# First LayerNorm's rows as background steps and a wider pace for the adaLN loads in a two-layer DiT kernel

## The chip, the cores and the metric

One core of a Trainium2 chip runs the kernel. The metric is the device time of one execution in microseconds, the median over several runs. An engine is one of the core's units: PE (TensorE, products), DVE (VectorE), ACT (ScalarE), POOL (GpSimd) and SP (SyncE, which here only issues DMAs).

## What is computed

The reference is two layers of a diffusion transformer block on 256 latent tokens and 256 context tokens with D = 1024. Cut to what the change touches:

```python
for l in range(DEPTH):                                        # DEPTH = 2
    mod_lat = silu(c) @ w_ada[l] + b_ada[l]                   # adaLN: 6 x 1024 shifts, scales and gates
    sh1, sc1, g1, sh2, sc2, g2 = split(mod_lat, 6)            # and the same for the context from c_ctx
    o_lat, o_ctx = token_mixer(x * (1 + sc1) + sh1, ...)      # attention, recurrence, output projection
    x = layernorm(ALPHA * x + g1 * o_lat, ln1_g[l], ln1_b[l])
    x = layernorm(ALPHA * x + g2 * mlp(x * (1 + sc2) + sh2), ln2_g[l], ln2_b[l])
    # mlp(h) = square(relu(h @ w_ff1)) @ w_ff2, hidden width 4096
    # in layer 0 the same two steps for the context; the output is the latent part after layer 1
```

## The kernel before, in words

**Tiles.** x is held as four blocks of 128 tokens (0 and 1 context, 2 and 3 latent), each as two halves of 128x512. Layer 0 works on all 512 tokens, layer 1's MLP on the 256 latent ones. Every product is made as three fp32r products of high and low halves (hi by hi, hi by lo, lo by hi). Weights come in units of 1 MB (tile `raw`): ACT casts a unit's four pieces to the high half `whi` (L120), DVE subtracts to the low half `wlo` (L128). Of `raw` there are three buffers, of split units two, so SP's next weight load waits until an earlier unit is split. A unit's split is emitted in four pieces between the matmuls of the unit before it.

**The MLP** (`mlp`, L1348). `f1(q, ns)` makes quarter q of the hidden layer in four units, transposed (`ps_cm`), and `ff1_evac` takes the relu and its square on ACT and splits it on DVE into `f_hi` and `f_lo` (L122 and L128). `f2(q)` multiplies a quarter by four units of the second matrix (`ps_tm`); where q < 3 it first calls f1 for one unit of the next quarter. In layer 0 a unit is 48 matmuls of 512 columns, 16 units in f1 and 16 in f2. The residual adds gate times result to x: L1180 (`res`) on DVE, L1181 (`x<-x,res`) on POOL, in the last quarter on DVE, with the statistics of the second LayerNorm behind (L1183).

**The first LayerNorm.** `ln_z` normalises x (L1219), `ln_t` transposes it on PE (`ps_z`), and `ln_h` makes the MLP's input h_hi and h_lo from that, with the rows g and b folded into scale and shift. The residual, though, needs x itself times g plus b. That is `ln_x` (L1249): it loads the rows g and b, each over 128 partitions (`ln_rows`, `ln_row` at L412), and for each half of a block emits a product (L1256) and a sum (L1257) on POOL, in place. In layer 0 that is 16 operations, in layer 1 eight. `mlp` calls it behind f1(0). `ln_x` also serves the second LayerNorm (`which == 2`), at the start of layer 1.

**adaLN.** The vectors of layer 1 are made in the background. `ada_queue` (L268) puts eight loads of 1 MB of w_ada (`raw_ada`, L275) into a queue, each with eight adds on DVE into eight accumulators (L290 for the first load, L292 after it); behind the eighth, `sums` makes 16 small matmuls (`ps_ada`), DVE adds the bias (L304, `ada_rows`), POOL scales the gate rows (L402) and PE transposes (`ps_adaT`). The table ADA starts two such queues at layer 0's MLP, 16 loads in all. `ada_step` is called when a unit begins; it emits the adds that are left, any sums that are due, and one load, if the planner's time has reached `ada_at`.

**What orders the work.** The planner counts PE time in `self.pe` (0.42 ns a column of a matmul). `tick`, called every three matmuls, emits a weight piece every third time, a step of the queue `bg` when `pe` has reached `bg_next`, and one ada add when it has reached `ada_next`. A step of `bg` has a cost; the next is emitted that much later. All of this sets the order of emission on each engine. At run time an instruction waits for its data, for its buffer and for its engine's earlier instructions, not for the planner's time.

```python
self.ada_at, self.ada_next, self.ada_gap = self.pe + pace, self.pe + 3000, (pace - 3000) / 8
```

Of the kernel before, what the change touches and what calls it, by code (L numbers as in the profile page):

```python
# [11 lines left out]
ALU = mybir.AluOpType  # L12
# [35 lines left out]
class Kern:  # L48
# [219 lines left out]
    def ada_queue(self, l, blocks, dve):  # L268
# [18 lines left out]
        def add(k, j, s):  # L287
            acc, w, c = st["acc"][s][j], st[k][:, j, :], self.silu[:, k, s:s + 1]
            if k == 0:
                self.nc.vector.tensor_scalar(acc, w, c, None, op0=ALU.mult)  # L290
            else:
                self.nc.vector.scalar_tensor_tensor(acc, w, c, acc, op0=ALU.mult, op1=ALU.add)  # L292
# [24 lines left out]
        for k in range(KD):  # L317
            if dve:
                self.ada_q.append((lambda k=k: dma(k),
                                   [lambda k=k, j=j, s=s: add(k, j, s) for j in range(4) for s in range(2)],  # L320
                                   sums if k == KD - 1 else None, self.ADA_PACE[l]))
            else:
                self.ada_q.append((lambda k=k: dma(k), [], lambda k=k: mms(k), 0.0))

    ADA_PACE = (9500, 10000)

    ADA = (('bra0',0,4,1),('bra0',0,8,1),('mlp0',1,0,1),('mlp0',1,4,1),('ga1',1,8,0))

# [919 lines left out]

    def ln_x(self, l, which):  # L1249

        nc = self.nc
        g, b = self.ln_rows(l, which)
        for tb in (range(4) if which == 1 and l == 0 else range(2, 4)):
            for hf in range(2):
                z = self.x[tb][hf]
                nc.gpsimd.tensor_tensor(z, z, g[hf], op=ALU.mult)  # L1256
                nc.gpsimd.tensor_tensor(z, z, b[hf], op=ALU.add)  # L1257
                if which == 2:
                    nc.sync.dma_start(out=self.xd[128 * (tb - 2):128 * (tb - 1), 512 * hf:512 * hf + 512], in_=z)

    def tail_units(self, l, which, keys, xs):

# [85 lines left out]
    def mlp(self, l):  # L1348
        cols = BOTH if l == 0 else LAT
        f = {}  # L1350

        def f1(q, ns=range(4)):
            for n in ns:
                w = self.take((l, "f1", q, n))
                for b in range(2):
                    p = self.cm_now(w, self.h, cols, b)
                    t = (self.g("f_hi", F32R), self.g("f_lo", F32R))
                    self.ff1_evac(p, cols, t)
                    f.setdefault(q, []).append(t)

        def f2(q, ns=range(2)):
            if q < 3:
                f1(q + 1, (0,))
            for n in ns:
                for h in range(2):
                    key = (l, "f2", q, n, h)
                    self.unit(key, self.take(key), f[q], self.tbs, q == 3)
            if q < 3:
                f.pop(q)
                f1(q + 1, (1, 2, 3))  # L1370

        self.start_residual(l, 2)
        if l == 0:

            ws = [self.take((l, "f1", 0, 0)), self.take((l, "f1", 0, 1), prefetch=False)]
            f[0] = [(self.g("f_hi", F32R), self.g("f_lo", F32R)) for _ in range(4)]
            for c in (CTX, LAT):
                for j in range(2):
                    if c is LAT and j:
                        self.prefetch()  # L1380
                    for b in range(2):
                        self.ff1_evac(self.cm_now(ws[j], self.h, c, b), c, f[0][2 * j + b])
                    if c is CTX and not j:
                        self.ln_late()
            f1(0, (2, 3))
        else:
            f1(0)
        self.ln_x(l, 1)
        for q in range(3):
            f2(q)  # L1390
        self.h = None
        f2(3, (0,))
        self.tail_units(l, 2, [(l, "f2", 3, 1, 0), (l, "f2", 3, 1, 1)], f[3])

# [174 lines left out]
```

## Time and profile before

| | before |
|---|---|
| median of 3 runs | 1557.56 us (1554.78 to 1559.41) |
| profiled execution | 1555.25 us |
| its span in the profile | 1553.4 us |
| PE busy | 1485.0 us, 96% |
| DVE busy | 1209 us, 78% |
| ACT busy | 723.8 us, 47% |
| POOL busy | 293.1 us, 19% |
| mean granted clock of PE | 0.979 |

The span is the stretch that the profile covers in the one execution that it recorded. Busy is the time in which an engine had an instruction in work; the granted clock is the share of full speed that TensorE had. Times in the trace count from the span's start. Layer 0's MLP runs from about 600 to 970 us, layer 1's from about 1363 us to the end.

### The profile page before, as it was taken

The page shows a single profiled execution, that of the slowest core. Times are in us where ns is not written, and L with a number is a line of the kernel's source. Part 1 is how long each engine was busy: PE and PEld are TensorE (multiplying, and loading weights), DVE is VectorE, ACT ScalarE, POOL GpSimd, SP SyncE. Part 2 cuts the span into 40 slices and gives each one's busy share as a digit, 9 for nine tenths or more (in the row PEclk, how much of TensorE's full clock was granted, in tenths as well). Part 3 has the DMA queues.
Part 4 walks back from the last instruction along what each step waited for, and adds up shares of the span by engine and source line. Part 5 has one row for each costly group of instructions (what it writes and reads, how often), then busy time and mean ns, then how long its engine had stood idle before and what let it go on. Part 6 is the DMA issues. An engine that isn't in the chain of part 4 may idle for free. (4 is left out here: it accounts for less than half of the span.)

```text
span 1553.4 us, 22377 instructions
## 1 busy us (share of the span) xinstructions
PE 1485.0 (96%) x8364; PEld 1231.1 (79%) x8364; DVE 1209.0 (78%) x2355; ACT 723.8 (47%) x1486; POOL 293.1 (19%) x302
## 2 busy tenths in 40 slices
PE   8799999999999999989999999899889999999997
PEld 4587988776878789866878888798777788898996
DVE  4799987849788869898984347988999756888667
ACT  2477766655224225312223232276577645555443
POOL 0532322100000002442030201445231000022110
PEclk9999999999999999989999999899899999999999
DMA  9522310014657544545552332252435723856553
GB/s 326 177 83 82 135 55 28 29 41 126 210 200 243 193 166 124 203 141 186 182 182 90 101 107 71 82 165 86 129 115 171 245 83 129 263 185 190 190 190 109
DMA packets 156750, 225.70 MB, mean 145 GB/s; under 512 B 5841, under 2 KB 118993, under 8 KB 151521
## 3 DMA queue, kind: packets, MB, share of 16 engines
q1 hardware_dynamic: 156640, 224.27, 43.9%
q8 instruction: 66, 1.08, 0.3%
q14 instruction: 44, 0.35, 0.1%
HBM read 218.97 MB, written 5.28 MB: 144 GB/s over the span
## 5 line engine op out<-in xcount | busy, mean ns | idle before, releaser
L128 DVE TENSOR_TENSOR wlo<-raw,whi 128x512 fp32r<-128x512 f32 x560 | 403.0, 744 | 119.4 <-ACT whi L120 113.6
L120 ACT CAST whi<-raw 128x512 fp32r<-128x512 f32 x483 | 275.5, 620 | 388.1 <-PE ps_tm L92 198.9
L92 PE MATMUL ps_cm<-h_hi,whi 128*128 128x256 f32 (+1 forms) x1216 | 412.7, 343 | 5.8 <-DVE whi L122 3.0
L92 PE MATMUL ps_cm<-h_hi,wlo 128*128 128x256 f32 (+1 forms) x1216 | 406.0, 336 | 3.2 <-DVE wlo L128 3.2
L92 PE MATMUL ps_cm<-h_lo,whi 128*128 128x256 f32 (+1 forms) x1216 | 406.9, 336 | 1.1 <-POOL h_lo L1241 0.8
L92 PEld LDWEIGHTS ps_cm<-h_hi,whi 128*128 128x128 f32 x1216 | 231.1, 191 | 48.8 <-issue 18.5
L92 PEld LDWEIGHTS ps_cm<-h_hi,wlo 128*128 128x128 f32 x1216 | 231.7, 191 | 27.9 <-DVE wlo L128 4.2
L92 PEld LDWEIGHTS ps_cm<-h_lo,whi 128*128 128x128 f32 x1216 | 232.4, 191 | 24.8 <-POOL h_lo L1241 2.4
L292 DVE SCALAR_TENSOR_TENSOR ada_acc<-raw_ada,silu,ada_acc 128x512 f32<-128x512 f32 x224 | 173.7, 820 | 26.7 <-DMA raw_ada<-in_w_ada_dram 26.5
L92 PE MATMUL ps_tm<-wlo,f_hi 128*128 128x512 f32 x384 | 150.8, 393 | 8.9 <-DVE wlo L128 8.9
L92 PE MATMUL ps_tm<-whi,f_hi 128*128 128x512 f32 x384 | 150.5, 392 | 0.0
L92 PE MATMUL ps_tm<-whi,f_lo 128*128 128x512 f32 x384 | 150.4, 392 | 0.0
L1181 POOL TENSOR_TENSOR x<-x,res 128x512 f32<-128x512 f32 x36 | 56.6, 1578 | 268.4 <-DVE res L1180 268.4
L92 PE MATMUL ps_tm<-wlo,h_hi 128*128 128x256 f32 x320 | 95.5, 298 | 8.0 <-DVE wlo L128 8.0
L92 PE MATMUL ps_tm<-whi,h_hi 128*128 128x256 f32 x320 | 96.9, 303 | 5.4 <-DVE whi L122 4.3
L92 PE MATMUL ps_tm<-whi,h_lo 128*128 128x256 f32 x320 | 94.4, 295 | 0.0
L92 PEld LDWEIGHTS ps_tm<-wlo,f_hi 128*128 128x128 f32 x384 | 72.8, 189 | 25.1 <-DVE wlo L128 10.2
L103 ACT ACTIVATE p<-ps_s,mx 128x512 f32<-128x512 f32 (+1 forms) x96 | 58.4, 615 | 57.8 <-DVE mx L993 29.9
L92 PEld LDWEIGHTS ps_tm<-whi,f_hi 128*128 128x128 f32 x384 | 72.7, 189 | 15.2
L92 PEld LDWEIGHTS ps_tm<-whi,f_lo 128*128 128x128 f32 x384 | 72.6, 189 | 15.1
L1241 POOL TENSOR_TENSOR h_lo<-hf,h_hi 128x256 fp32r<-128x256 f32 x28 | 23.4, 843 | 268.9 <-DVE h_hi L1240 267.8
L92 PEld LDWEIGHTS ps_tm<-wlo,h_hi 128*128 128x128 f32 x320 | 65.1, 204 | 10.6 <-DVE wlo L128 9.8
(171 smaller groups left out, 2509.8 us busy)
## 6 DMA issues: line engine op xcount, KB each, us to landing
raw<-in_w_ff_dram SPq DMA_DIRECT2D x64, 1024.0 KB, 5.5
raw<-in_w_in_dram SPq DMA_DIRECT2D x50, 1024.0 KB, 5.0
raw_ada<-in_w_ada_dram SPq DMA_DIRECT2D x40, 1024.0 KB, 4.9
w_ada<-in_w_ada_dram SPq DMA_DIRECT2D x32, 256.0 KB, 5.7
raw<-in_w_br_c_dram SPq DMA_DIRECT2D x8, 1024.0 KB, 5.2
raw<-in_w_out_dram SPq DMA_DIRECT2D x8, 1024.0 KB, 5.4
gw_raw<-in_v_gate_dram SPq DMA_DIRECT2D x16, 256.0 KB, 5.3
raw<-in_w_br_a_dram SPq DMA_DIRECT2D x8, 512.0 KB
```

The source lines that it names most:

```text
L92: self.nc.tensor.matmul(out, lhsT, rhs, start=start, stop=stop, **kw)
L103: ins = self.nc.scalar.activation(out, in_, func, **kw).ins
L120: self.nc.scalar.copy(out, in_)
L128: self.nc.vector.tensor_tensor(lo, src, hi.bitcast(F32), op=ALU.subtract)
L292: self.nc.vector.scalar_tensor_tensor(acc, w, c, acc, op0=ALU.mult, op1=ALU.add)
L1181: (nc.vector if last else nc.gpsimd).tensor_tensor(x, x, t, op=ALU.add)
L1241: last = (nc.gpsimd if s == 0 or k % 2 else nc.vector).tensor_tensor(lo[:, c], h, hi[:, c].bitcast(F32), op=ALU.subtract)
```

## The change

`ln_x` for the first LayerNorm no longer emits its operations at once: it appends each as a step of cost 2000 to `bg`, and is called ahead of f1 (in layer 0 ahead of its third and fourth unit, in layer 1 ahead of the first) instead of behind it. f1's first unit of quarter 1 is taken out of `f2(0)` and stands before it, and behind it the steps that are left are emitted (`drain_bg`). The order of PE's products stays as it was. The pace of layer 1's loads of w_ada goes from 10000 to 18000.

```diff
-    ADA_PACE = (9500, 10000)
+    ADA_PACE = (9500, 18000)
...
         for tb in (range(4) if which == 1 and l == 0 else range(2, 4)):
             for hf in range(2):
                 z = self.x[tb][hf]
+                if which == 1:
+                    for row, op in ((g[hf], ALU.mult), (b[hf], ALU.add)):
+                        self.bg.append((2000, lambda z=z, row=row, op=op: nc.gpsimd.tensor_tensor(z, z, row, op=op), False))
+                    continue
                 nc.gpsimd.tensor_tensor(z, z, g[hf], op=ALU.mult)
                 nc.gpsimd.tensor_tensor(z, z, b[hf], op=ALU.add)
-                if which == 2:
-                    nc.sync.dma_start(out=self.xd[128 * (tb - 2):128 * (tb - 1), 512 * hf:512 * hf + 512], in_=z)
+                nc.sync.dma_start(out=self.xd[128 * (tb - 2):128 * (tb - 1), 512 * hf:512 * hf + 512], in_=z)
...
         def f2(q, ns=range(2)):
-            if q < 3:
+            if 0 < q < 3:
                 f1(q + 1, (0,))
...
+            self.ln_x(l, 1)
             f1(0, (2, 3))
         else:
+            self.ln_x(l, 1)
             f1(0)
-        self.ln_x(l, 1)
         for q in range(3):
+            if q == 0:
+                f1(1, (0,))
+                self.drain_bg()
             f2(q)
```

In the changed file the first LayerNorm's operations have line 1259, those of the second 1261 and 1262.

SP's queue in the first half of layer 0's MLP, before. `raw` of 128x8x256 is a unit of f1, of 128x4x512 one of f2; the pair in the fourth row is f1(0)'s last unit and the unit of f1(1, (0,)).

```order
L275 DMA raw_ada<-in_w_ada_dram 128x2048
L412 DMA gate<-gd 128x512 x4
L275 DMA raw_ada<-in_w_ada_dram 128x2048
L186 DMA raw<-in_w_ff_dram 128x8x256 x2
L275 DMA raw_ada<-in_w_ada_dram 128x2048
L186 DMA raw<-in_w_ff_dram 128x4x512
L275 DMA raw_ada<-in_w_ada_dram 128x2048
L186 DMA raw<-in_w_ff_dram 128x4x512
L412 DMA ln_row<-in_ln_g_dram 128x512 x2
L412 DMA ln_row<-in_ln_b_dram 128x512 x2
```

And the same place of the changed kernel:

```order
L275 DMA raw_ada<-in_w_ada_dram 128x2048
L412 DMA gate<-gd 128x512 x4
L186 DMA raw<-in_w_ff_dram 128x8x256
L275 DMA raw_ada<-in_w_ada_dram 128x2048
L186 DMA raw<-in_w_ff_dram 128x8x256
L412 DMA ln_row<-in_ln_g_dram 128x512 x2
L412 DMA ln_row<-in_ln_b_dram 128x512 x2
L186 DMA raw<-in_w_ff_dram 128x4x512
L275 DMA raw_ada<-in_w_ada_dram 128x2048
L186 DMA raw<-in_w_ff_dram 128x4x512 x2
```

The rows' loads have moved ahead of two weight loads of f2 and two of w_ada, and a w_ada load now stands at every second weight load.

POOL from the end of `ln_h` to the start of layer 1, with what is taken out and put in:

```order
 L1241 TENSOR_TENSOR h_lo<-hf,h_hi 128x256 x12
-L1256 TENSOR_TENSOR x<-x,ln_row 128x512 x4
-L1257 TENSOR_TENSOR x<-x,ln_row 128x512 x4
-L1256 TENSOR_TENSOR x<-x,ln_row 128x512 x2
-L1257 TENSOR_TENSOR x<-x,ln_row 128x512 x2
-L1256 TENSOR_TENSOR x<-x,ln_row 128x512 x2
-L1257 TENSOR_TENSOR x<-x,ln_row 128x512 x2
-L1181 TENSOR_TENSOR x<-x,res 128x512 x16
+L1259 TENSOR_TENSOR x<-x,ln_row 128x512 x16
+L1181 TENSOR_TENSOR x<-x,res 128x512 x24
```

The sixteen products and sums have one line now; they stand between the same neighbours. The gate rows' product (L402), which stood among the residuals' sums, now follows them.

DVE around f1(1, (0,)) and the first units of f2, before. The adds are those of the w_ada loads; the first wlo is the last piece of f2's first unit, the next three are of its second:

```order
L128 TENSOR_TENSOR wlo<-raw,whi 128x512
L292 SCALAR_TENSOR_TENSOR ada_acc<-raw_ada,silu,ada_acc 128x512 x4
L122 CAST f_hi<-relu 128x512
L292 SCALAR_TENSOR_TENSOR ada_acc<-raw_ada,silu,ada_acc 128x512
L128 TENSOR_TENSOR f_lo<-relu,f_hi 128x512
L292 SCALAR_TENSOR_TENSOR ada_acc<-raw_ada,silu,ada_acc 128x512
L128 TENSOR_TENSOR wlo<-raw,whi 128x512 x2
L122 CAST f_hi<-relu 128x512
L128 TENSOR_TENSOR wlo<-raw,whi 128x512
```

And of the changed kernel, where the first four wlo are those of f1(1, (0,)) and the last two the first of f2; five adds and an f_hi stand ahead of the piece:

```order
L128 TENSOR_TENSOR f_lo<-relu,f_hi 128x512
L128 TENSOR_TENSOR wlo<-raw,whi 128x512 x2
L122 CAST f_hi<-relu 128x512
L292 SCALAR_TENSOR_TENSOR ada_acc<-raw_ada,silu,ada_acc 128x512
L128 TENSOR_TENSOR f_lo<-relu,f_hi 128x512
L128 TENSOR_TENSOR wlo<-raw,whi 128x512 x2
L292 SCALAR_TENSOR_TENSOR ada_acc<-raw_ada,silu,ada_acc 128x512 x3
L122 CAST f_hi<-relu 128x512
L292 SCALAR_TENSOR_TENSOR ada_acc<-raw_ada,silu,ada_acc 128x512
L128 TENSOR_TENSOR f_lo<-relu,f_hi 128x512
L292 SCALAR_TENSOR_TENSOR ada_acc<-raw_ada,silu,ada_acc 128x512 x3
L128 TENSOR_TENSOR wlo<-raw,whi 128x512 x2
```

The eight adds of a load are now spread over two units instead of one.

## Rows read from the trace of the kernel before

**Rows 1.** Page, part 1: busy us (share of the span) and instructions of each engine.

```profile
PE 1485.0 (96%) x8364; PEld 1231.1 (79%) x8364; DVE 1209.0 (78%) x2355; ACT 723.8 (47%) x1486; POOL 293.1 (19%) x302
```

**Rows 2.** PE's waits, 590 to 1060 us: us in total, times, longest us.

```profile
PE ps_tm L92 <- DVE wlo L128: 8.3, 3, 5.7
PE ps_ada L92 <- DVE ada_acc L292: 4.0, 4, 2.7
```

**Rows 3.** PE's timeline, 659 to 677 us: start, us, instruction [idle before <-releaser].

```profile
659.77 0.39 PE L92 MATMUL ps_tm<-whi,f_hi 128*128 128x512 f32 x1
...
662.49 0.39 PE L92 MATMUL ps_tm<-whi,f_hi 128*128 128x512 f32 x1
664.52 0.50 PE L92 MATMUL ps_tm<-wlo,f_hi 128*128 128x512 f32 x1 [1.64 <-DVE wlo L128]
...
671.21 0.80 PE L92 MATMUL ps_tm<-wlo,f_hi 128*128 128x512 f32 x1 [5.73 <-DVE wlo L128]
...
676.46 0.39 PE L92 MATMUL ps_tm<-wlo,f_hi 128*128 128x512 f32 x1
```

**Rows 4.** Windows: us, PE, PEld, DVE, ACT, POOL busy (instructions), PEclk, DMA share, GB/s.

```profile
660.00:670.00 10.00, 3.84 (x16) 2.55 (x14) 10.00 (x7) 2.18 (x4) 10.00 (x7) 0.81 0.00 0
670.00:680.00 10.00, 8.79 (x28) 7.06 (x29) 8.27 (x13) 0.00 (x0) 0.61 (x1) 0.68 0.63 210
...
700.00:710.00 10.00, 7.05 (x33) 3.65 (x32) 9.52 (x14) 2.18 (x4) 1.74 (x2) 1.00 0.58 183
```

**Rows 5.** POOL's timeline, 630 to 672 us, first and last of six rows.

```profile
643.90 6.97 POOL L1256 TENSOR_TENSOR x<-x,ln_row 128x512 f32<-128x512 f32 x4 [35.35 <-DMA ln_row<-in_ln_g_dram]
...
667.23 3.37 POOL L1257 TENSOR_TENSOR x<-x,ln_row 128x512 f32<-128x512 f32 x2
```

**Rows 6.** DVE's timeline, adds ahead of that stretch and in it.

```profile
639.20 2.08 DVE L292 SCALAR_TENSOR_TENSOR ada_acc<-raw_ada,silu,ada_acc 128x512 f32<-128x512 f32 x3 [1.88 <-DMA raw_ada<-in_w_ada_dram]
...
644.54 6.89 DVE L292 SCALAR_TENSOR_TENSOR ada_acc<-raw_ada,silu,ada_acc 128x512 f32<-128x512 f32 x4
```

**Rows 7.** SP's timeline, 610 to 660 us: issue of DMAs.

```profile
612.32 5.96 SPq L186 DMA_DIRECT2D raw<-in_w_ff_dram  x2
...
636.21 0.37 SPq L186 DMA_DIRECT2D raw<-in_w_ff_dram  x1
636.67 0.93 SPq L412 DMA_DIRECT2D ln_row<-in_ln_g_dram  x2
```

**Rows 8.** PE's timeline, first matmuls of both adaLN sums and of the products behind.

```profile
704.23 1.05 PE L92 MATMUL ps_ada<-ada_acc,pick 128*32 128x512 f32 x4
...
711.51 0.50 PE L92 MATMUL ps_cm<-h_hi,whi 128*128 128x512 f32 x1
...
799.27 1.06 PE L92 MATMUL ps_ada<-ada_acc,pick 128*32 128x512 f32 x6
...
803.05 0.50 PE L92 MATMUL ps_cm<-h_hi,whi 128*128 128x512 f32 x1
```

**Rows 9.** PE's timeline, sums of an earlier adaLN queue, 441 to 446 us.

```profile
442.49 1.93 PE L92 MATMUL ps_ada<-ada_acc,pick 128*32 128x512 f32 x16
```

**Rows 10.** DVE's timeline, last residuals of layer 0's MLP, 935 to 962 us.

```profile
950.75 0.69 DVE L1180 TENSOR_TENSOR res<-ps_tm,gate 128x512 f32<-128x512 f32 x1 [1.14 <-PE ps_tm L92]
```

**Rows 11.** Windows at the start of layer 1, columns as in rows 4.

```profile
1000.00:1008.00 8.00, 4.52 (x19) 4.23 (x20) 8.00 (x11) 0.00 (x0) 4.71 (x4) 0.54 0.01 2
```

**Rows 12.** SP's timeline, start of layer 1's MLP.

```profile
1355.06 1.26 SPq L412 DMA_DIRECT2D gate<-gd  x2
```

**Rows 13.** POOL's timeline, layer 1's first MLP product, 1355 to 1410 us.

```profile
1368.44 1.05 POOL L1241 TENSOR_TENSOR h_lo<-hf,h_hi 128x256 fp32r<-128x256 f32 x1 [1.23 <-DVE h_hi L1240]
1390.53 6.28 POOL L1256 TENSOR_TENSOR x<-x,ln_row 128x512 f32<-128x512 f32 x4 [21.03 <-DMA ln_row<-in_ln_g_dram]
```

**Rows 14.** Windows in layer 1's first MLP product, columns as in rows 4.

```profile
1368.00:1380.00 12.00, 12.00 (x102) 11.96 (x101) 10.80 (x23) 7.71 (x18) 1.05 (x1) 1.00 0.53 176
...
1390.00:1404.00 14.00, 12.42 (x65) 10.34 (x65) 13.15 (x12) 5.40 (x12) 12.38 (x8) 1.00 0.44 140
```

## The prediction, made before the result

> **What bounds the kernel now.** I read the shares of busy time first: PE is busy 96% of a span of 1553.4 us, DVE 78%, POOL 19% [rows 1]. So the end is set by TensorE's own work wherever it never waits, and the change can give back only what PE waits for in the two MLPs. The second view, PE's waits over layer 0's MLP and the start of layer 1, names the two kinds that the change can touch: 8.3 us for low halves of weights (wlo), 5.7 of it in one piece, and 4.0 us for ada_acc [rows 2].
>
> Where the first lies is seen in PE's timeline. Up to 662.49 a matmul follows the other every 0.227 us (twelve from 659.77). From 662.49 on, sixteen take until 676.46, with 5.73 us of waiting for wlo ahead of the one at 671.21 [rows 3]; they should take 3.63 and take 13.97. **The loss is 10.3 us.** It is not waiting alone: 1.64 at 664.52 and the 5.73 leave 2.9 us, and the two windows there show a granted clock of 0.81 and 0.68 on the mean of 10 us, so part of them ran at the lower level of 1.2 GHz [rows 4].
>
> The cause is seen in the timelines of POOL and DVE. Sixteen products and sums of the first LayerNorm's rows run on POOL without a gap from 643.90 to 670.6, 26.7 us or 1.67 each [rows 5]. In that time four adds on DVE take 6.89, 1.72 each; just before, three took 2.08, or 0.69 each [rows 6]. About 16 DVE operations lie beside the 16 of POOL, so **each POOL operation costs DVE about 1.0 us, 16 in all**, and that puts wlo behind PE. That the burst does not come earlier is SP's queue: the first ln_row loads are issued at 636.67, right behind a weight load at 636.21 [rows 7], and POOL had waited 35.35 us for them [rows 5].
>
> **Layer 0's rows.** The edit paces these operations in the order of emission, but nothing in the changed order holds them back at run time. POOL's sequence is the same sixteen in a row between the same neighbours, and none waits for a matmul of the MLP's product; they wait for the ln_rows, for the transposes of x and for each other. What moves is the loads: now right behind the weights of f1(1,0), four transfers earlier. Those weights were the second of the pair on which SP spent 612.32 to 618.28 [rows 7]. From the issue to POOL's start it took 643.90 - 636.67 = 7.2 us, so the burst should go from about 625 to 652: under f1's last unit and f1(1,0) instead of f1(1,0) and f2.
>
> The Trainium skill, "SBUF — State Buffer", in its part on the shared port pair, says that a DVE operation with two SBUF inputs and one of GpSimd hold one pair of ports exclusively, the loser waiting for a whole instruction. By that rule sixteen operations cost DVE their 16 us however they are spread, and the sum is the one below; if spacing them out made them free, the whole 10.3 would come back. The trace has 1.72 against 0.69 in a dense burst and no spaced one.
>
> I lay the changed DVE order over the burst at 1.69 us an operation. Three adds, f_hi, f_lo and two wlo of f1(1,0) end at 636.5; f_hi, an add, f_lo and its last two wlo at 643.3 and 645. A unit is 48 matmuls of 0.227, or 10.9 us, and 662.49 is the sixth of f2's second unit, so f1(1,0) starts near 639.5 and wants those two pieces at matmuls 12 and 18, near 642.2 and 643.6: 0.9 us late in all once the first wait has shifted the rest. Three adds and f_hi use up the burst. At 0.69 each, an add, f_lo, three adds and the first wlo of f2 then end near 655, where PE wants it at 651.5: 3.4 late. That unit's last two are 0.7 late, and the next unit's, behind four adds that wait for their load, 0.9. Together 5.9 against 10.3: **-4.4 us**. The ends are -10.3 (nothing late) and 0 (the same loss again). I take the middle, since half as many adds are emitted per unit, while the burst still fills DVE. A wait of 3.4 lies between one of 5.73 that the lower clock followed and the 2.7 for ada_acc [rows 2] that it did not (1.00 in that window [rows 4]); it could cost up to 2.9 more.
>
> **The pace.** A unit of 512 columns counts 10.3 us in the planner's time, so a pace of 10 made one load per unit and 18 makes one in every second unit. The 16 loads and their 128 adds remain; but the gap grows from 875 to 1875 ns, the last add is emitted 3 + 7 x 1.875 = 16.1 us into a stretch of 20.6, and the sums behind find it done. Before, they did not: the first sums ran from 704.23 to the next product at 711.51, the second from 799.27 to 803.05 [rows 8]. Sixteen that wait for nothing took 1.93 us [rows 9]. So (7.28 - 1.93) + (3.78 - 1.93) = 7.2 us were lost, 4.0 of them in waits that the profile counts, the rest where a chunk had to start anew. I take **-7.2 us**, with 4.0 and, if the adds are late again, 0 as other ends.
>
> **What it costs.** The loads now end with the MLP, so eight adds (5.5 us) fall among the last residuals, four of them, 2.8 us, ahead of the last unit's wlo. DVE waits up to 1.14 us for PE there [rows 10], which takes half: **+1.3 us**, between 0 and 2.8. The second sums move into the start of layer 1, where DVE is busy 8.00 of 8 us and PE 4.52 at a clock of 0.54 [rows 11]. Their 1.93 us on PE fall into its idle time; what counts is DVE's row add, 0.69: **+0.7 us**, with -1.9 if PE's share is a gain there. A product on POOL (gate_rows) goes between h_lo and delays nothing that the order shows on PE.
>
> **Layer 1's rows.** Eight operations start at 1390.53, four in 6.28 us [rows 13]. Their loads now follow the gate rows of 1355.06 [rows 12] without the four weight loads between, land before h_lo ends at 1369.5, and the burst follows h_lo there, to about 1382. DVE is busy 10.80 of 12 us in that stretch; in the old one 13.15 of 14, and PE lost 1.58 [rows 14]. Eight operations bring 8 us where 1.2 is free, and what is late can be worked off in the units behind: I estimate a wait of 2.8 in place of 1.58, **+1.2 us**, between -1.6 and +8.7 (a stall like layer 0's, 10.3 - 1.6).
>
> SP has the same number of transfers; ln_row now stands ahead of the first f2 unit's weights instead of the third's, and adds 2 us of issue there (two pairs at 0.93 [rows 7]), which a unit of 10.9 hides. ACT's casts and PE's products are the same.
>
> **Sum.** -4.4 - 7.2 + 1.3 + 0.7 + 1.2 = -8.4 us. The profiled execution took 1555.25, 1.85 over its span, so it would take 1546.9; it lies 2.3 below the median of the runs shown, and from 1557.56 the same step gives **1549.2 us**. A measurement of this kernel can tell about 0.3%, 4.7 us, from no change.
>
> **Rivals.**
> 1. *Everything goes.* With four adds and four wlo in 10.9 us of f2, DVE is half free and hides the burst; 10.3, 7.2 and layer 1's 1.6 vanish against 2.0 of costs (tail and start of layer 1): -17.1, 1540.5. For it: DVE's mean share is 78% [rows 1]. Against it: beside POOL's burst DVE is full with any sixteen operations.
> 2. *The stall only moves.* wlo starves one unit earlier for the same 10.3, and half the gain at the sums is lost because their adds queue behind the late wlo: -3.6 + 2.0 = -1.6, 1556.0. For it: POOL's sequence and price are unchanged.
> 3. *Slower: two stalls instead of one.* f1 makes f_hi and f_lo on DVE besides wlo, so the burst makes PE wait long in f1(1,0) and again in f2, each time with the lower clock behind: 20.6 in place of 10.3, -7.2 and 3.2 of costs, +6.3 and 1563.9. It decides at PE's wait near 642: above some 2.7 us it costs the clock too. For it: PE at 0.54 behind the second LayerNorm's burst [rows 11]. Against it: the 0.9 that my layout gives.
> 4. *The change does not do what it says.* That the pace of POOL's operations has no effect at run time is in my forecast already. If it had one, sixteen steps of 2 us would make the burst 32 us instead of 26.7 at the same price, and the wait near 655 would shrink; it goes with rival 1 then.
>
> **How the numbers follow.** The forecast has 0.50, its own range from 1544 to 1554; 0.43 is faster by over 0.3%, 0.07 within. Rival 1, with 4, has 0.15, all faster. Rival 2 has 0.18, all within. Rival 3 has 0.17, 0.15 slower and 0.02 within. Faster 0.58, same 0.27, slower 0.15. The range from 1540 to 1560 reaches from rival 1 past rival 2 and leaves out most of rival 3 and a little below.
>
> **What would show it.** POOL's sixteen start near 625 without gaps at 1.6 to 1.7 each, DVE's operations beside them take 1.7, and PE waits for wlo near 642 and 651 to 655, at most 3.4 at once. No wait for ada_acc is left. In layer 1 POOL's eight start behind h_lo. I am wrong if POOL's operations are spread out, if the waits near 651 are absent or above 6 us, or if the tail or layer 1's f1 waits over 4.

## The result and the profile after

| | before | after |
|---|---|---|
| median | 1558.49 us (1554.78 to 1560.55, 4 runs) | 1540.01 us (1539.24 to 1541.43, 4 runs) |
| ratio, 95% interval | | 0.9897, 0.9877 to 0.9918 |
| profiled execution | 1555.25 us | 1539.24 us |
| its span | 1553.4 us | 1537.5 us |

The change makes the kernel 18.5 us faster by the medians and 16.0 by the profiled executions. The kernel before scatters by 6 us, and later groups of it had medians from 1554.5 to 1556.0 us; beside those the gain is 14.5 to 16.0. Forecast were 8.4 us: the sign is right and the size half. The median lies below the 1544 to 1554 of the forecast itself, and only 0.01 us inside the stated range of 1540 to 1560; that it is inside at all is luck.

The profile says where it came from. PE is busy for 5.3 us less than in [rows 1], with the same instructions; the page of the changed kernel:

```profile
PE 1479.7 (96%) x8364; PEld 1228.2 (80%) x8364; DVE 1205.0 (78%) x2355; ACT 724.4 (47%) x1486; POOL 293.0 (19%) x302
```

PE's waits over the same stretch as [rows 2]:

```profile
PE ps_tm L92 <- DVE wlo L128: 6.2, 5, 3.1
PE ps_cm L92 <- DVE whi L122: 3.7, 1, 3.7
PE ps_cm L92 <- DVE wlo L128: 2.0, 2, 1.8
```

No wait for ada_acc is left, and the longest for wlo fell from 5.7 to 3.1. PE's timeline in place of [rows 3]:

```profile
648.39 0.39 PE L92 MATMUL ps_tm<-whi,f_hi 128*128 128x512 f32 x1
651.89 0.66 PE L92 MATMUL ps_tm<-wlo,f_hi 128*128 128x512 f32 x1 [3.12 <-DVE wlo L128]
...
655.64 0.39 PE L92 MATMUL ps_tm<-wlo,f_hi 128*128 128x512 f32 x1
```

Ten matmuls from 648.39 should take 2.27 us and take 7.25. The stall costs 5.0 us now, 3.12 of it waiting; the rest is the lower clock, as in the window behind it, 0.52, near the half that is 1.2 GHz:

```profile
652.00:654.00 2.00, 2.00 (x5) 1.58 (x6) 1.97 (x4) 0.00 (x0) 0.00 (x0) 0.52 0.72 170
```

SP, POOL and DVE, in place of [rows 5 to 7], in three views:

```profile
613.97 0.38 SPq L186 DMA_DIRECT2D raw<-in_w_ff_dram  x1
614.40 1.05 SPq L412 DMA_DIRECT2D ln_row<-in_ln_g_dram  x2
```

```profile
621.51 27.86 POOL L1259 TENSOR_TENSOR x<-x,ln_row 128x512 f32<-128x512 f32 x16 [14.81 <-DMA ln_row<-in_ln_g_dram]
```

```profile
619.99 3.40 DVE L292 SCALAR_TENSOR_TENSOR ada_acc<-raw_ada,silu,ada_acc 128x512 f32<-128x512 f32 x5
...
634.83 3.47 DVE L128 TENSOR_TENSOR wlo<-raw,whi 128x512 fp32r<-128x512 f32 x2
638.22 5.18 DVE L292 SCALAR_TENSOR_TENSOR ada_acc<-raw_ada,silu,ada_acc 128x512 f32<-128x512 f32 x3
...
651.16 1.28 DVE L128 TENSOR_TENSOR wlo<-raw,whi 128x512 fp32r<-128x512 f32 x2
```

Sixteen operations run on POOL without a gap, 1.74 us each, the moment the rows have landed. The steps of cost 2000 do not show. DVE's operations beside them take 1.73 us as before, and the wlo of f2's first unit comes at 651.16, behind the burst, which ends at 649.37, and three adds. The sums, in place of [rows 8], wait for nothing; PE's timeline:

```profile
773.72 1.92 PE L92 MATMUL ps_ada<-ada_acc,pick 128*32 128x512 f32 x16
775.58 0.50 PE L92 MATMUL ps_tm<-whi,f_hi 128*128 128x512 f32 x1
...
952.95 1.92 PE L92 MATMUL ps_ada<-ada_acc,pick 128*32 128x512 f32 x16
954.80 0.39 PE L92 MATMUL ps_cm<-h_hi,whi 128*128 128x256 f32 x1
```

The second sum now stands behind layer 0's MLP. In layer 1 the burst follows h_lo, in place of [rows 13], and PE waits twice beside it; POOL's and PE's timelines:

```profile
1352.48 13.00 POOL L1259 TENSOR_TENSOR x<-x,ln_row 128x512 f32<-128x512 f32 x8
```

```profile
1361.65 0.39 PE L92 MATMUL ps_cm<-h_hi,wlo 128*128 128x256 f32 x1 [0.39 <-DVE wlo L128]
...
1366.74 0.39 PE L92 MATMUL ps_cm<-h_hi,wlo 128*128 128x256 f32 x1 [1.24 <-DVE wlo L128]
```

**Stage by stage.** Three landmarks cut the span: the first h_lo on POOL (583.26 us before, 582.07 after), the last f_lo product of layer 0's MLP (968.84, 952.63) and the first h_lo of layer 1's MLP (1363.74, 1346.78). They give the three lengths that the table below has for every kernel. Up to the first landmark no kernel differs in its program, and it lay between 582.1 and 587.2; so the lengths tell more than the totals. Each is from one profiled execution. In the first length, the six kernels without rows on POOL at the pace of 18000 lie within 0.3 us of each other; in the mixer, six kernels with the same order of work there (after, pace only, loads early, no rows wide, and rows on DVE at the wide pace with steps and without) lie between 392.5 and 395.3. Of the 15.9 us of span, **15.0 lie in layer 0's MLP**, 0.7 in layer 1's mixer, -1.1 in layer 1's MLP, and 1.2 ahead of everything that was changed.

| kernel | median, us | ratio, 95% interval | layer 0's MLP | layer 1's mixer | layer 1's MLP to end |
|---|---|---|---|---|---|
| before | 1558.49 | | 385.6 | 394.9 | 189.7 |
| after | 1540.01 | 0.9897 (0.9877 to 0.9918) | 370.6 | 394.2 | 190.7 |
| pace only | 1542.54 | 0.9918 (0.9900 to 0.9936) | 371.2 | 393.0 | 190.3 |
| rows' move only | 1554.68 | 0.9997 (0.9986 to 1.0008) | 386.3 | 395.6 | 190.7 |
| loads early, no steps | 1540.96 | 0.9906 (0.9889 to 0.9923) | 370.5 | 394.6 | 190.7 |
| sums one unit later | 1552.55 | 0.9975 (0.9963 to 0.9988) | 380.4 | 394.1 | 190.3 |
| no rows, wide pace | 1533.15 | 0.9852 (0.9828 to 0.9876) | 364.7 | 392.5 | 188.4 |
| no rows, old pace | 1542.52 | 0.9910 (0.9892 to 0.9929) | 371.2 | 395.8 | 188.1 |
| rows on DVE, wide pace | 1533.23 | 0.9858 (0.9840 to 0.9876) | 364.7 | 395.3 | 187.8 |
| rows on DVE, old pace | 1540.89 | 0.9910 (0.9893 to 0.9928) | 372.4 | 396.0 | 188.0 |
| rows on DVE, no steps | 1533.81 | 0.9863 (0.9845 to 0.9881) | 364.8 | 392.7 | 188.4 |
| both norms on DVE, later | 1534.34 | 0.9857 (0.9838 to 0.9875) | 364.9 | 398.1 | 187.7 |
| both norms on DVE, steps | 1533.11 | 0.9853 (0.9832 to 0.9875) | 364.8 | 394.7 | 189.3 |
| **both norms on DVE, direct** | **1527.03** | 0.9816 (0.9799 to 0.9832) | 365.0 | 389.2 | 187.8 |

Each ratio is against the runs of the kernel before on the same chip.

### The profile page after: what moved, and what is told of

It is laid out like the page before. It is cut to its first block, busy times and chain, and to the rows that moved or that the text cites. A ratio compares the mean times of both kernels' runs of the same rounds, so it can differ in the third digit from the quotient of the medians.

```text
span 1537.5 us, 22376 instructions
## 1 busy us (share of the span) xinstructions
PE 1479.7 (96%) x8364; PEld 1228.2 (80%) x8364; DVE 1205.0 (78%) x2355; ACT 724.4 (47%) x1486; POOL 293.0 (19%) x302
## 5 line engine op out<-in xcount | busy, mean ns | idle before, releaser
L292 DVE SCALAR_TENSOR_TENSOR ada_acc<-raw_ada,silu,ada_acc 128x512 f32<-128x512 f32 x224 | 166.5, 790 | 50.1 <-DMA raw_ada<-in_w_ada_dram 49.9
L1181 POOL TENSOR_TENSOR x<-x,res 128x512 f32<-128x512 f32 x36 | 51.9, 1445 | 303.8 <-DVE res L1180 303.8
L92 PEld LDWEIGHTS ps_tm<-whi,f_hi 128*128 128x128 f32 x384 | 72.5, 189 | 15.9 <-ACT whi L120 0.8
L676 POOL TENSOR_TENSOR lru_i<-lru_i,xc 128x512 f32<-128x512 f32 x32 | 56.7, 1798 | 88.9 <-ACT lru_i L103 87.6
```

What stands on the lines that cost most here:

```text
L92: self.nc.tensor.matmul(out, lhsT, rhs, start=start, stop=stop, **kw)
L676: nc.gpsimd.tensor_tensor(ig, ig, self.xc[k[0]][0], op=ALU.mult)
L1181: (nc.vector if last else nc.gpsimd).tensor_tensor(x, x, t, op=ALU.add)
```

## The experiments

The theory was that the pace and the moved loads are two gains, and that the steps do nothing on POOL. The first three kernels take the change apart.

**Pace only.**

```diff
-    ADA_PACE = (9500, 10000)
+    ADA_PACE = (9500, 18000)
```

> The kernel before with one edit, the pace of layer 1's adaLN loads 10000 -> 18000; the LayerNorm rows stay where they were. Theory A (two separate gains: the pace frees the sums of their waits, some 7.3 us, and the earlier loads move POOL's burst): the sums' waits are gone; the sixteen POOL operations start later than before, near 659 us, because fewer w_ada loads stand between the weight loads, and lie beside f2 with half the adds, so PE's wait for wlo there is between 0 and 5 us; layer 1's wait of 1.6 us stays. 1541 to 1546 us beside a kernel before at 1558. Theory B (the earlier loads are what lifts the long stall): the stall of 10.3 us stays and only the sums gain, 1551. Theory C (the background steps of cost 2000 matter at run time): as B.

Measured: 1542.54 us. In the MLP of layer 0 the pace alone does 14.4 of the 15.0 us. The burst starts at 648.93 and not at 659, 5 us from its old place [rows 5], and only 1.4 us counted from the first landmark; yet in place of the stall of 10.3 us there are three waits of 4.2 us in all. POOL's and PE's timelines:

```profile
648.93 5.67 POOL L1256 TENSOR_TENSOR x<-x,ln_row 128x512 f32<-128x512 f32 x4 [37.41 <-DMA ln_row<-in_ln_g_dram]
```

```profile
668.05 0.50 PE L92 MATMUL ps_tm<-wlo,f_hi 128*128 128x512 f32 x1 [1.53 <-DVE wlo L128]
...
690.27 0.50 PE L92 MATMUL ps_tm<-wlo,f_hi 128*128 128x512 f32 x1 [2.20 <-DVE wlo L128]
...
691.95 0.79 PE L92 MATMUL ps_tm<-wlo,f_hi 128*128 128x512 f32 x1 [0.44 <-DVE wlo L128]
```

Theory B, that the earlier loads lift the stall, is out: with four adds per unit instead of eight, DVE gets most of its wlo through a burst at nearly the same place. The burst is not free, though: this stage is 6.5 us longer than without the rows (371.2 - 364.7, below).

**The rows' move only.** The changed kernel with

```diff
-    ADA_PACE = (9500, 18000)
+    ADA_PACE = (9500, 10000)
```

> The changed kernel with the pace put back to 10000: only the LayerNorm rows move. Theory A: the sums wait as before (7.3 us lost), and the burst lies beside f1 with all eight adds per unit, so PE's stall for wlo is 5 to 12 us: 1553 to 1560, about the kernel before. Theory B: the stall shrinks to the 5 us of the changed kernel with the sums as before: 1552. Theory C: the stall is gone because the steps are spread, 1548.

Measured: 1554.68, no difference, in theory A's range. The stall does shrink, to some 6.5 us (thirteen matmuls from 651.85 take until 661.35, 9.5 us in place of 2.95), but the adds that DVE did not get to come out at the first sum. PE's timeline:

```profile
655.76 0.79 PE L92 MATMUL ps_tm<-wlo,f_hi 128*128 128x512 f32 x1 [3.52 <-DVE wlo L128]
...
704.19 1.06 PE L92 MATMUL ps_ada<-ada_acc,pick 128*32 128x512 f32 x6
709.37 3.45 PE L92 MATMUL ps_ada<-ada_acc,pick 128*32 128x512 f32 x10 [4.12 <-DVE ada_acc L292]
```

The longest wait there, 2.7 before [rows 2], has become 4.12. So DVE's arrears, the work that it is late with, do not vanish when the burst moves; they travel to the next place where PE wants something of DVE.

**Loads early, no steps.** Pace 18000, the rows loaded at the new place, the POOL operations emitted at once at the old one:

```diff
+            rows = self.ln_rows(l, 1)
             f1(0, (2, 3))
         else:
+            rows = self.ln_rows(l, 1)
             f1(0)
-        self.ln_x(l, 1)
+        self.ln_x(l, 1, rows)
```

> The kernel before with pace 18000 and with the four ln_row loads issued where the changed kernel issues them, but the products and sums on POOL emitted at once at their old place and not as background steps. Theories A and B: POOL's sequence and SP's queue are those of the changed kernel, so the time is the changed kernel's 1540 within 2 us, and the burst starts near 621 us and lasts 27 us. Theory C: without the steps the stall of 10 us is back, 1545 or more.

Measured: 1540.96 and the changed kernel's lengths within 0.5 us. POOL's timeline has the same burst without the steps, sixteen operations until 649.61:

```profile
623.06 6.67 POOL L1256 TENSOR_TENSOR x<-x,ln_row 128x512 f32<-128x512 f32 x4 [14.24 <-DMA ln_row<-in_ln_g_dram]
```

The steps have no effect on POOL, theory C is out. What is left of the move, beside the kernel with the pace alone, is 0.7 us in layer 0's MLP and 1.6 us of median: not separable from its scatter.

The next kernels ask what the sums' wait and the rows are worth by themselves.

**Sums one unit later**, at the old pace and with the rows at the old place:

```diff
+        late, self.ada_late = getattr(self, "ada_late", None), None
+        if late is not None:
+            late()
         if self.ada_pend is not None:
-            self.ada_pend()
+            if self.ada_acc:
+                self.ada_late = self.ada_pend
+            else:
+                self.ada_pend()
...
             load, adds, self.ada_pend, pace = self.ada_q.pop(0)
+            self.ada_acc = pace == 10000
```

> The kernel before with pace 10000 and the rows at their old place; the only edit is that each of the two layer-1 adaLN sums in layer 0's MLP is emitted one unit later, so that its adds are done when PE reaches it. Theory A1 (the sums' waits are worth 7.2 us by themselves): 1548 to 1549 beside a kernel before at 1556. Theory A2 (the adds stay as dense as before, and what PE doesn't lose at the sums it loses at the wlo queued behind the same adds; only fewer adds per unit help): 1553 to 1556.

Measured: 1552.55, and layer 0's MLP 5.2 us shorter. Both sums run through without a wait, 7.3 us less, but PE now waits for wlo where it did not; its timeline:

```profile
787.06 0.50 PE L92 MATMUL ps_tm<-wlo,f_hi 128*128 128x512 f32 x1 [0.29 <-DVE wlo L128]
788.75 0.50 PE L92 MATMUL ps_tm<-wlo,f_hi 128*128 128x512 f32 x1 [0.73 <-DVE wlo L128]
```

The time lies between the ranges of A1 and A2, and both are half right: with eight adds per unit a part comes back behind the sums.

**No rows**, at both paces. These kernels leave the first LayerNorm's g and b out of the residual's x, in both layers; the edit at pace 18000, and the same at 10000:

```diff
-        self.ln_x(l, 1)
```

> Pace 18000, and the first LayerNorm's products and sums, and their loads, left out in both layers (x goes into the MLP's residual without g and b, so a part of the computation is left out). What the rows still cost in the changed kernel: by its trace 5.0 us in layer 0 and 1.6 in layer 1, so 1533 to 1534, as the kernel with the rows on DVE. If the operations on DVE still cost something, this is 1 to 3 us below that one's 1533.2.

> The same omission at the old pace of 10000. By the trace of the kernel before the rows cost 10.3 us in layer 0 and 1.6 in layer 1, so 1544 beside 1556. Theory A (the pace is worth 7.2 us at the sums and nothing else): 7 us above the wide one without rows, 1541. Rival E (the pace alone took 13 us off because with half the adds per unit the burst costs less; without a burst only the sums are left): the same 7. If the difference between narrow and wide is 13 here too, the pace has a gain of its own that has nothing to do with the burst.

Measured: 1533.15 and 1542.52. Neither theory had 9.4 us between them. Without a burst the first sums at the old pace take 2.3 us, near the 1.93 without a wait, and the second still wait; PE's timeline:

```profile
693.22 2.40 PE L92 MATMUL ps_ada<-ada_acc,pick 128*32 128x512 f32 x16
...
783.33 1.06 PE L92 MATMUL ps_ada<-ada_acc,pick 128*32 128x512 f32 x6
786.20 1.90 PE L92 MATMUL ps_ada<-ada_acc,pick 128*32 128x512 f32 x10 [1.81 <-DVE ada_acc L292]
```

So nearly all of the 5.4 us that the first sums lost were the burst's arrears, 34 us behind its end, and not the pace's own; the second sums' wait is the pace's. And 6.5 of the 9.4 lie in layer 0's MLP, where 1.9 is the second sum that the wide pace moves behind it, where it costs nothing that can be seen: the mixer is not longer for it. The rest is a mixer 3.3 us shorter, about what the mixer varies by.

**Rows on DVE**, the changed kernel with one word in its steps:

```diff
-                        self.bg.append((2000, lambda z=z, row=row, op=op: nc.gpsimd.tensor_tensor(z, z, row, op=op), False))
+                        self.bg.append((2000, lambda z=z, row=row, op=op: nc.vector.tensor_tensor(z, z, row, op=op), False))
```

> The changed kernel with the first LayerNorm's products and sums on DVE instead of POOL, in the same background steps of cost 2000. On DVE the order of emission is an order at run time, so here the steps are spread between the other work, at 0.69 us each instead of 1.0 us of DVE time lost beside each POOL operation (24 operations: 16.6 us instead of 24). Theory A: PE's waits near 651 us (5 us with the slow clock) go, in layer 1's f1 a wait of 0 to 2 us stays: 1533 to 1537 us. Rival D (DVE is the limit in those stretches whoever has the operations): DVE's queue puts wlo as late as before, 1540 to 1545.

Measured: 1533.23, as without any rows; rival D is out. The operations take 0.69 us, their neighbours are back at 0.6 to 0.76, and DVE has them all in time; DVE's timeline, and the windows of that stretch with PE at 20.00 of 20:

```profile
633.71 2.50 DVE L1259 TENSOR_TENSOR x<-x,ln_row 128x512 f32<-128x512 f32 x4
...
639.04 0.70 DVE L1259 TENSOR_TENSOR x<-x,ln_row 128x512 f32<-128x512 f32 x1
```

```profile
620.00:640.00 20.00, 20.00 (x90) 16.57 (x89) 19.51 (x34) 6.90 (x13) 0.00 (x0) 1.00 0.61 213
640.00:660.00 20.00, 20.00 (x90) 16.58 (x89) 18.53 (x31) 6.35 (x12) 0.00 (x0) 1.00 0.46 159
```

DVE is 19 of 20 us busy there with the rows, and PE never waits. Beside leaving them out, having POOL do them costs 5.9 us of this stage at this pace (370.6 - 364.7) and 14.4 at the old one (385.6 - 371.2). The two kernels that follow ask whether the pace or the steps matter once POOL is out of it; their edits are the pace put back to 10000, and `nc.vector` for the first norm in the kernel with early loads, at the old place:

```diff
-                nc.gpsimd.tensor_tensor(z, z, g[hf], op=ALU.mult)
-                nc.gpsimd.tensor_tensor(z, z, b[hf], op=ALU.add)
+                e = nc.vector if which == 1 else nc.gpsimd
+                e.tensor_tensor(z, z, g[hf], op=ALU.mult)
+                e.tensor_tensor(z, z, b[hf], op=ALU.add)
```

> The first LayerNorm's rows on DVE in steps, at the old pace of 10000. Theory A (the rows' loss and the pace's gain are two things): without the burst on POOL the kernel is where the one without rows stood at this pace, 1542.5, plus 0 to 5 us because DVE now has eight adds, four wlo, two f_hi, two f_lo and some six row operations in a unit of f1, about 10 of 10.9 us: 1542 to 1548. Theory F (DVE is what is short and only fewer adds help): as the kernel before, 1553 or more.

> Pace 18000, row loads early, the first LayerNorm's operations on DVE but emitted at once at the old place instead of in steps of cost 2000: sixteen in one run, 11 us of DVE, between the weight pieces. Theory G (on DVE the steps matter, since its order is the order at run time): the next unit's wlo come up to 9 us late against one unit of slack, PE waits 2 to 6 us there with the slow clock: 1536 to 1542 against 1533.2 in steps. Theory H (a unit of slack of 10.9 us covers a run of 11 us; only the place on DVE matters, not the steps): 1533 to 1535.

Measured: 1540.89 and 1533.81. At the old pace the rows on DVE give what the wide pace gives with the rows on POOL, a little below theory A's 1542 to 1548; theory F is out. PE waits for no wlo there, but the first sums take 6.1 us (7.28 before, 2.3 without rows), so the rows leave arrears on DVE too where the adds are dense. PE's timeline:

```profile
693.70 1.05 PE L92 MATMUL ps_ada<-ada_acc,pick 128*32 128x512 f32 x4
...
699.81 0.50 PE L92 MATMUL ps_cm<-h_hi,whi 128*128 128x512 f32 x1
```

Without steps nothing is lost, as theory H has it. That does not settle G, which has them matter: the run of sixteen never came about, since the compiled DVE sequence had the operations in groups of one to four between the others.

**The second norm too.** With the first norm's rows gone from POOL, the largest stall left is the second LayerNorm's burst at the start of layer 1 [rows 11]. The first kernel moved its eight operations to DVE in steps (the branch for `which == 1` taken for both norms, with the four stores of x as steps of cost 100) and its call behind `finish(0)`, the first recurrence batch; the second has the steps with the call at its old place; the third emits them there directly:

```diff
-                nc.gpsimd.tensor_tensor(z, z, g[hf], op=ALU.mult)
-                nc.gpsimd.tensor_tensor(z, z, b[hf], op=ALU.add)
+                nc.vector.tensor_tensor(z, z, g[hf], op=ALU.mult)
+                nc.vector.tensor_tensor(z, z, b[hf], op=ALU.add)
```

> The kernel with the first LayerNorm's rows on DVE in steps, and the second LayerNorm's eight operations at the start of layer 1 too on DVE, in steps behind the first recurrence batch instead of in one run on POOL. Theory: the burst there (978 to 989 us in the changed kernel, DVE full, PE waiting 3.7 and 1.8 us and at the low clock behind it, some 9 us lost) goes, 1525 to 1529. Rival: DVE is full in that stretch without the burst, and the operations only move to another stretch in which DVE is full: 1531 to 1536.

> As the kernel with both norms' rows on DVE, but the second LayerNorm's steps put into the queue at their old place, ahead of the first recurrence batch instead of behind it. In the one behind it the waits of the burst (some 10 us for whi and wlo at the start of layer 1) were gone, but a wait of 9.9 us for ACT's yr had come later. Theory: that wait came from the moved place (two edits in one kernel), and here it is gone: 1525 to 1529. Rival: the stretch from layer 1's start to its attention has one length set by DVE and ACT together, and a wait of some 10 us comes in any case: 1531 to 1535.

> As the kernel with the first LayerNorm's rows on DVE in steps, and the second LayerNorm's eight operations on DVE too, emitted directly at their old place and in no queue: 5.5 us of DVE in place of some 8 lost beside POOL. Theory: DVE is full there, so PE gains the difference and part of the time at the low clock, 2 to 5 us: 1528 to 1531. Rival: no gain, 1533 to 1535, since the wait for DVE at layer 1's start only moves.

Measured: 1534.34, 1533.11 and **1527.03**; the first two lie where their rivals had them, the third a little below its theory. In all three PE's 5.8 us of waiting for whi and wlo in the first products of layer 1 (`ps_cm`) are gone but for 0.2. In the two with steps a wait for ACT's yr takes their place; PE's waits in the mixer of the second:

```profile
PE ps_gate L92 <- ACT yr L103: 10.7, 2, 9.9
```

It came with the steps, at either place of the call. ACT's timelines show where ACT loses the time; the second kernel, then the third:

```profile
998.25 0.27 ACT L932 COPY v<-ps_tm 128x128 f32<-128x128 f32 x1 [7.77 <-PE ps_tm L92]
...
1007.21 2.57 ACT L103 ACTIVATE lru_th<-lru_r,sp 128x512 f32<-128x512 f32 x4
```

```profile
990.15 2.60 ACT L103 ACTIVATE lru_th<-lru_r,sp 128x512 f32<-128x512 f32 x4
```

In the second kernel ACT's part of the recurrence (`lru_th` and what follows it) stands behind copies that wait for PE, and starts 17 us later; yr comes behind it. The recurrence emits its own steps through the same queue `bg`, so steps put in there can change the order on another engine; that this is the reason was not tried. The direct kernel does not have the wait, and its mixer is 5 us shorter than that of the changed kernel and 3.3 below the shortest of the six named above. It is the fastest of all, 28.8 us below the kernel before on its chip (1555.84).

## Why the prediction was right in sign and half the size

- **What bounds the kernel** held: layer 0's MLP gave 15.0 of the 15.9 us, by fewer waits of PE and less of the lower clock.
- **No pacing on POOL** held to the letter: sixteen in a row from 621.51, 27.86 us, and a kernel without steps takes the same time.
- **Layer 0's rows, -4.4 us:** the stall went from 10.3 to 5.0, so -5.3; the size held, the reason only in part. The layout gave it to the moved loads and to half as many adds per unit together. The pace alone turns the stall into waits of 4.2 us in all; the move alone shortens it to some 6.5 and gives nothing at the end. The layout also had the first wait near 642, 0.9 us; it did not come, since the adds that it put into the burst had run ahead of it.
- **The pace, -7.2 us:** the sums lost 7.2 and lose none, as worked out. But that was priced as if the pace's gap made the waits. The kernel without rows shows that the first sums' wait was nearly all the burst's backlog, so this term and the one above are not two separate gains.
- **The step that failed in size is the costs of the wide pace: two ends were not taken**, each of them named: the second sum's 1.9 us of PE, moved to where PE idles (counted as none), and the tail (+1.3, came to none: PE does not wait between the last residuals). DVE's row add at layer 1's start (+0.7) is not to be seen either; the mixer came out 0.7 us shorter, within what it varies from kernel to kernel. Together 1.9 + 1.3 + 1.4 = 4.6 us. The stall was 0.9 better than laid out, and the first two units, where fewer adds stand, gave 0.7 (594.52 against 593.33 at their first relu, 623.25 against 621.39 at f1's third; the same 0.7 lies between all kernels looked at with either pace). With 1.2 us ahead of the MLP, not the change's, that makes 7.4 of the 7.6 by which 16.0 exceeds 8.4. Of this the mixer's 0.7 and the 1.2 are scatter, so the sum closes better than its terms are known.
- **Layer 1's rows, +1.2 us:** the stage is 1.1 longer than before, but 0.4 longer than in the kernels with the pace alone or the sums later, whose rows stand at the old place too; no more than 0.4 to 1.1 can be said. The waits are 0.39 and 1.24 us in place of 1.58, and not the 2.8 laid out. Without the rows the stage takes 188.1 to 188.4.
- **The rivals.** The first, everything goes, came nearest the time (1540.5), but the burst's stall did not go; the time agrees because of the ends above. The second, that a stall only moves, is close to what the move alone does. The third asked for a first long wait near 642, which was not there.

The Trainium skill's rule on the shared port pair ("SBUF — State Buffer") was weighed as a price that no spreading lowers. No run spreads the rows on POOL, but the changed kernel's trace has single POOL operations among DVE's, and there it agrees; POOL's and DVE's timelines:

```profile
680.59 1.73 POOL L1181 TENSOR_TENSOR x<-x,res 128x512 f32<-128x512 f32 x1 [5.39 <-DVE res L1180]
```

```profile
680.42 3.10 DVE L292 SCALAR_TENSOR_TENSOR ada_acc<-raw_ada,silu,ada_acc 128x512 f32<-128x512 f32 x3
```

Three adds beside one POOL operation take 3.10 us, and alone 2.08 [rows 6]: 1.0 more, as in the burst. The runs show one thing more. What a GpSimd operation takes from DVE here, about 1.0 us, exceeds what the same operation costs on DVE itself, 0.69, so taking it off DVE loads DVE more.

## What to carry to other kernels

Ask of a step queue which engine it orders and whether anything there waits for the paced clock; on an engine whose inputs are all there, the steps become a burst as soon as the loads land, and here the loads' place in the DMA queue was what set its time. Where one engine is in arrears, price the arrears and not the waits: they appear wherever the main engine next asks, and a remedy for one wait (earlier rows, later sums) sends them, in part or whole, to the next. And before giving elementwise work to GpSimd to relieve VectorE, read how long VectorE's own operations take beside it.

## What the runs showed of the hardware that was not expected

- A product or sum of 128x512 floats on POOL (1.3 us alone, up to 1.74 in the burst) makes a DVE product or sum of that size beside it take 1.6 to 1.8 us instead of 0.69, the cast f_hi 1.5 instead of 0.42. The same operation on DVE takes 0.69. Twenty-four of them moved to DVE made the kernel as fast as with none.
- A wait of 3.12 us was followed by the lower clock (0.52 in the next window of 2 us); two waits of 2.20 and 0.44 close together by 0.73 in the 6 us around them; the longest of before's first sums, 2.7 [rows 2], by none, with 1.00 [rows 4]. So the lower clock followed stalls much shorter than the 5.73 of [rows 3].

```profile
688.00:694.00 6.00, 3.36 (x9) 2.15 (x9) 6.00 (x9) 1.83 (x4) 1.59 (x1) 0.73 0.01 3
```

That row is the window of the kernel with the pace alone, columns as in [rows 4].
